# Holding back GpSimd's cast loads in a sparse 3x3 convolution until the weights are on chip

## Chip, cores, metric

One core of one Trainium2 chip. The metric is the device time of one execution in microseconds (us). A profile gives a span, from the first to the last instruction, that is 1.7 to 1.8 us shorter than the time of the same execution.

## The reference

```python
x:      (16, 64, 64, 64)  float32
weight: (128, 64, 3, 3)   float32, about 90% of it zero
x_pad = np.pad(x, ((0, 0), (0, 0), (1, 1), (1, 1)))
output[b, co] = sum over ci, kh, kw of weight[co, ci, kh, kw] * x_pad[b, ci, kh:kh+64, kw:kw+64]
# output: (16, 128, 64, 64) float32
```

The kernel takes no advantage of the zeros and computes a dense convolution in bf16. It reads 17 MB and writes 33.5 MB.

## The kernel before

Images go in eight pairs, 64 channels of each on 128 partitions. Three kinds of loads stand at the start. The SP queue brings the weights and the first 36 rows of pair 0 in fp32 (`x_head`, in two pieces of 9 and 27 rows), which VectorE and ScalarE cast to bf16. GpSimd brings everything else with loads that cast on the way.

```python
nc.sync.dma_start(out=w_sb, in_=weight...)
x_head = const_pool.tile([128, HEAD, W], FP32, name="x_head")          # HEAD = 36
for a, b in ((0, 9), (9, HEAD)):
    nc.sync.dma_start(out=x_head[:, a:b, :], in_=pair(0)[:, a:b, :])
nc.gpsimd.dma_start(out=xs[0][:, HEAD:H, :], in_=pair(0)[:, HEAD:H, :])  # tail of pair 0
...
for p in range(1, NP):
    nc.gpsimd.dma_start(out=xs[p], in_=pair(p))                          # seven more pairs
... # 27 matmuls of zeros, casts and transposes of the weights
cast_x(nc.vector.tensor_copy, 0, 9)      # x_head, first piece
cast_x(nc.scalar.copy, 9, 18)            # x_head, second piece
cast_x(nc.vector.tensor_copy, 18, HEAD)
```

The first 16 rows are two "direct" blocks of 18 matmuls. All other blocks take two output rows at once: GpSimd adds neighbouring rows into `s`, TensorE makes products, and VectorE adds two of them into `o`. When both `o` tiles of a pair are complete, SP stores them (2.1 MB each; the last pair goes in four stores of 1 MB).

## Time and profile before

| | before |
|---|---|
| median of the first three runs | 132.42 us (132.15 to 132.76) |
| span of the trace | 130.3 us |
| second piece of x_head on chip | 13.96 us |
| TensorE without a gap | 14.71 to 117.10 us |
| last addition into o ends | 119.64 us |

The record calls the profiled run (132.03 us) slow. There is only one core, so no second die to hold it against, and the runs beside it took as long. A second trace of the same kernel stands among the experiments (b_again).

These are three rows of the page's table of 40 equal slices, each of 3.26 us here: the clock granted to TensorE in tenths of full speed, the busy share of the 16 DMA engines in tenths, and the GB/s that they wrote.

```profile
PEclk9985559999999999999999999999999999999655
DMA  4999999999999999999999999999599929999990
GB/s 136 217 297 228 216 209 226 209 216 216 302 325 307 327 322 314 362 428 438 423 425 428 433 423 433 428 428 443 244 408 403 403 86 402 458 385 415 415 410 18
```

Two things are to be seen. TensorE has half its clock from the fourth slice to the sixth, around its wait for x_head. The DMA engines are full from the second slice on except in two places late in the kernel, a 5 and a 2, with 244 and 86 GB/s. Such a place, where the engines have too little to do, is called a hole below; its size is the length of the stage times what the share lacks of 1.

### The profile page before, as it was taken

The page shows a single profiled execution, that of the slowest core. Times are in us where ns is not written, and L with a number is a line of the kernel's source. Part 1 is how long each engine was busy: PE and PEld are TensorE (multiplying, and loading weights), DVE is VectorE, ACT ScalarE, POOL GpSimd, SP SyncE. Part 2 cuts the span into 40 slices and gives each one's busy share as a digit, 9 for nine tenths or more (in the row PEclk, how much of TensorE's full clock was granted, in tenths as well). Part 3 has the DMA queues.
Part 4 walks back from the last instruction along what each step waited for, and adds up shares of the span by engine and source line. Part 5 has one row for each costly group of instructions (what it writes and reads, how often), then busy time and mean ns, then how long its engine had stood idle before and what let it go on. Part 6 is the DMA issues. An engine that isn't in the chain of part 4 may idle for free.

```text
span 130.3 us, 2488 instructions
## 1 busy us (share of the span) xinstructions
PE 110.6 (85%) x1002; PEld 56.0 (43%) x1002; DVE 83.0 (64%) x136; ACT 38.0 (29%) x70; POOL 40.7 (31%) x45
## 2 busy tenths in 40 slices
PE   6662499999999999999999999999999999993000
PEld 6430144445444544454445445544544454440000
DVE  0350425778777868787777777777777777777000
ACT  3500313333333333333243333333333333330000
POOL 6900463333333333333333333324333330000000
PEclk9985559999999999999999999999999999999655
DMA  4999999999999999999999999999599929999990
GB/s 136 217 297 228 216 209 226 209 216 216 302 325 307 327 322 314 362 428 438 423 425 428 433 423 433 428 428 443 244 408 403 403 86 402 458 385 415 415 410 18
DMA packets 4188, 42.99 MB, mean 330 GB/s; under 512 B 464, under 2 KB 464, under 8 KB 976
## 3 DMA queue, kind: packets, MB, share of 16 engines
q1 hardware_dynamic: 3024, 35.03, 64.6%
q0 software_dynamic: 1152, 7.80, 29.1%
q8 instruction: 8, 0.13, 0.4%
q14 instruction: 4, 0.03, 0.1%
HBM read 17.07 MB, written 33.55 MB: 389 GB/s over the span
## 4 chain that ended last, share of the span: by engine, by line
PE 79%; DMA 9%; DVE 1%; issue 1%; SPq 1%; ACT 1%; DVEq 0%
PE ps L136 79%; DMA x_head<-in_x_dram 9%; DVE o L169 1%; ACT x L88 1%; DVEq L215 0%; SPq L63 0%; SPq L60 0%; DVEq L169 0%
## 5 line engine op out<-in xcount | busy, mean ns | idle before, releaser
L136 PE MATMUL ps<-x,wT 64*128 64x504 bf16 (+3 forms) x780 | 91.4, 381 | 6.7 <-ACT x L88 4.2
L169 DVE TENSOR_TENSOR o<-ps,pc 128x512 f32<-128x512 f32 x124 | 77.8, 686 | 22.4 <-PE ps L136 20.1
L136 PEld LDWEIGHTS <-wT 64*128 64x128 bf16 x966 | 52.4, 96 | 60.4 <-issue 10.4
L155 POOL TENSOR_TENSOR s<-x 128x512 bf16<-128x512 bf16 x31 | 35.6, 1152 | 65.6 <-PE ps L136 43.4
L162 ACT COPY pc<-ps 128x512 f32<-128x512 f32 x62 | 33.3, 589 | 64.3 <-issue 61.8
L136 PE MATMUL ps<-s,wT 64*128 64x512 bf16 (+1 forms) x186 | 25.8, 380 | 0.0
L88 DVE CAST x<-x_head 128x576 bf16<-128x576 f32 (+1 forms) x2 | 1.2, 611 | 7.5 <-DMA x_head<-in_x_dram 7.5
L75 PE MATMUL ps<-idle_rhs 128*128 128x128 bf16 x27 | 3.1, 313 | 1.0 <-DVE idle_rhs L72 1.0
L68 POOL DMA_DIRECT2D x<-in_x_dram x7 | 3.7, 551 | 0.0
L150 DVE COPY o<-ps 128x512 f32<-128x512 f32 x2 | 1.4, 688 | 3.4 <-PE ps L136 3.4
L75 PEld LDWEIGHTS <-idle_rhs 128*128 128x128 bf16 x27 | 2.8, 149 | 1.0 <-DVE idle_rhs L72 1.0
L88 ACT CAST x<-x_head 128x576 bf16<-128x576 f32 x1 | 0.7, 672 | 8.2 <-DMA x_head<-in_x_dram 8.2
L92 DVE CAST w_bf<-w_sb 128x192 bf16<-128x192 f32 (+1 forms) x4 | 1.2, 360 | 2.5 <-DMA w_sb<-in_weight_dram 2.5
L149 ACT COPY o<-ps 128x512 f32<-128x512 f32 x2 | 1.2, 582 | 3.6 <-PE ps L136 3.6
L92 ACT ACT_TABLE_LOAD x1 | 1.3, 1283 | 0.7 <-PEq L204 0.7
L98 PE MATMUL ps<-ident,w_bf 128*128 128x128 bf16 x9 | 1.2, 308 | 0.0
L92 ACT CAST w_bf<-w_sb 128x64 bf16<-128x64 f32 (+1 forms) x2 | 0.7, 417 | 1.4 <-DMA w_sb<-in_weight_dram 1.4
L102 DVE TENSOR_TENSOR wT<-ps,wT 128x384 bf16<-128x384 f32 x2 | 1.0, 549 | 0.0
L98 PEld LDWEIGHTS <-w_bf 128*128 128x128 bf16 x9 | 0.8, 130 | 0.4 <-DVE w_bf L92 0.4
L64 POOL DMA_DIRECT2D x<-in_x_dram x1 | 0.7, 696 | 0.8 <-POOLq L204 0.8
L72 DVE MEMSET idle_rhs<- 128x64 uint32 x1 | 0.1, 112 | 0.8 <-PEq L204 0.8
L111 ACT CAST wT<-ps 128x384 bf16<-128x384 f32 x1 | 0.5, 478 | 0.4 <-PE ps L98 0.4
(8 smaller groups left out, 1.9 us busy)
## 6 DMA issues: line engine op xcount, KB each, us to landing
out_dram<-o SPq DMA_DIRECT2D x14, 2048.0 KB, 14.4
x<-in_x_dram POOLq DMA_DIRECT2D x7, 1024.0 KB, 26.1
out_dram<-o SPq DMA_DIRECT2D x4, 1024.0 KB, 9.4
x_head<-in_x_dram SPq DMA_DIRECT2D x1, 864.0 KB, 12.3
x<-in_x_dram POOLq DMA_DIRECT2D x1, 448.0 KB, 8.8
w_sb<-in_weight_dram SPq DMA_DIRECT2D x1, 288.0 KB, 2.7
x_head<-in_x_dram SPq DMA_DIRECT2D x1, 288.0 KB, 6.0
```

The lines of the kernel that those rows point to most:

```text
L68: nc.gpsimd.dma_start(out=xs[p], in_=pair(p))
L75: nc.tensor.matmul(idle_ps, idle_rhs, idle_rhs, start=True, stop=True)
L88: copy(out=xs[0][:, a:b, :], in_=x_head[:, a:b, :])
L92: copy(out=w_bf4[:, g, a:b, :], in_=w_v[:, k : k + b - a, :])
L98: nc.tensor.matmul(wps[:, j, :], src, ident, start=True, stop=True)
L102: nc.vector.tensor_tensor(out=wT[:, g], in0=wps, in1=wT[:, G1], op=SUB)
L136: nc.tensor.matmul(ps[n][:, lo:hi, c_lo:c_hi], tap(g, kw, n), src[q, a:b:step, c_lo + kw - 1 : c_hi + kw - 1], start=(i == 0), stop=(i == ...
L149: nc.scalar.copy(out=o[0][:, r0 : r0 + rows, :], in_=ps[0])
L150: nc.vector.tensor_copy(out=o[1][:, r0 : r0 + rows, :], in_=ps[1])
L155: nc.gpsimd.tensor_tensor(out=s, in0=xs[p][:, r0 : r0 + 16 : 2, :], in1=xs[p][:, r0 + 1 : r0 + 16 : 2, :], op=ADD)
L162: nc.scalar.copy(out=c, in_=shared[n])
L169: nc.vector.tensor_tensor(out=o[n][:, first : r0 + 16 : 2, :], in0=ps[n], in1=pc[n], op=ADD)
```

## The change

Its intent: GpSimd issues its cast loads only when the weights are there, so that the weights and x_head have the DMA engines to themselves. To make GpSimd wait for the weights, it takes over one of the small casts.

```diff
-    nc.gpsimd.dma_start(out=xs[0][:, HEAD:H, :], in_=pair(0)[:, HEAD:H, :])
     ident = const_pool.tile([128, 128], BF16, name="ident")
     make_identity(nc, ident)
-    for p in range(1, NP):
-        nc.gpsimd.dma_start(out=xs[p], in_=pair(p))
 ...
     cast(G2, nc.scalar.copy, 0, 3)
-    cast(G2, nc.vector.tensor_copy, 3, 4)
+    cast(G2, nc.gpsimd.tensor_copy, 3, 4)
+
+    nc.gpsimd.dma_start(out=xs[0][:, HEAD:H, :], in_=pair(0)[:, HEAD:H, :])
+    for p in range(1, NP):
+        nc.gpsimd.dma_start(out=xs[p], in_=pair(p))
```

## The prediction

> **What bounds the kernel now.** I read the page's slice table first, then the chain that ended last, then the start in the timeline, then the stages with DMA share. The chain of waits names one wait only, at the start:
>
> ```profile
> 1.65 12.31 DMA x_head<-in_x_dram
> 13.96 0.02 issue
> 13.98 0.68 ACT x L88
> 14.66 0.04 issue
> 14.71 102.39 PE ps L136 x936
> ```
>
> The columns are start and length in us. After the second piece of x_head has landed at 13.96, TensorE works without a gap until 117.10. So the start looks like pure loss, and a chain read alone would promise all of it back. Section 6 of the page says why that piece takes so long:
>
> ```profile
> x_head<-in_x_dram SPq DMA_DIRECT2D x1, 864.0 KB, 12.3
> x<-in_x_dram POOLq DMA_DIRECT2D x1, 448.0 KB, 8.8
> w_sb<-in_weight_dram SPq DMA_DIRECT2D x1, 288.0 KB, 2.7
> x_head<-in_x_dram SPq DMA_DIRECT2D x1, 288.0 KB, 6.0
> ```
>
> Read the last column, us from issue to landing. 288 KB of weights take 2.7, the same amount of x_head behind them 6.0: from 3.5 us on GpSimd's cast loads share the engines. The chain stops at compute, so the DMA needs a look of its own. In this answer by stages the last three columns are the granted clock, the DMA engines' busy share and GB/s:
>
> ```profile
> 20.00:33.00 13.00, 13.00 (x126) 6.50 (x123) 9.92 (x16) 4.45 (x10) 4.80 (x5) 1.00 1.04 214
> 33.00:57.00 24.00, 24.00 (x228) 11.98 (x226) 18.42 (x31) 8.10 (x16) 8.82 (x8) 1.00 1.01 333
> 57.00:91.00 34.00, 34.00 (x320) 16.98 (x318) 26.84 (x43) 11.52 (x22) 12.21 (x11) 1.00 1.01 429
> 91.00:95.00 4.00, 4.00 (x42) 2.02 (x38) 2.87 (x5) 1.37 (x3) 1.62 (x2) 1.00 0.66 272
> 95.00:104.00 9.00, 9.00 (x86) 4.49 (x84) 7.17 (x12) 3.12 (x6) 3.17 (x3) 1.00 0.99 415
> 104.00:107.00 3.00, 3.00 (x34) 1.52 (x30) 2.48 (x4) 0.91 (x3) 0.99 (x2) 1.00 0.04 11
> 107.00:127.00 20.00, 11.28 (x106) 5.43 (x102) 10.04 (x16) 3.48 (x7) 0.45 (x1) 0.86 1.00 418
> ```
>
> The DMA engines are full almost throughout. GB/s counts what is written, so a cast load from fp32 to bf16 shows 214 while it reads twice that, 428, the same as the 429 of pure stores: **some 428 GB/s of the wider side is the ceiling here**. The page gives 17.07 MB read and 33.55 MB written, 50.6 MB, or 118 us of a 130 us span. The engines run dry in just two places, because the outputs are not computed yet: 91 to 95 (4 x 0.35 = 1.4 us) and 104 to 107 (2.9 us). So this kernel has two bounds nearly level: late compute, and the bytes.
>
> **What the Trainium skill says.** "DMA: Bandwidth & Descriptors", section "Issuing engines are not separate DMA queues", says that DMAs of all issuers run on the same 16 engines and interleave; its section "Queues, rings and completion order" says that each engine goes round-robin between queues packet by packet. The trace agrees: 6.0 us against 2.7 us for 288 KB. "TensorE: Matmul & The Clock Gate", section "What's actually happening", says that the array's clock halves after an idle window of about 3.4 us and needs as long a busy one to recover. The trace agrees: after the gap from 10.49 to 14.71 the 18 matmuls of the second direct block take 4.02 us, those of the first, partly at full clock, 2.77. "SBUF — State Buffer", section "SBUF: two separate sides", says that some VectorE copies lock GpSimd out of the port that it writes descriptors through. The trace does not show it: GpSimd's seven issues keep to 535 to 563 ns each though VectorE casts from 3.46 to 4.63.
>
> **The change, part by part.**
> Removed from the start: the 448 KB load (issued at 1.23) and seven loads of 1024 KB (2.46 to 6.19). Added to GpSimd: one cast of 128x64 elements, taken from VectorE, where the smallest cast of that group took 0.21 us. GpSimd took 1.15 us for a two-input add of 128x512, so an eighth of the elements should cost 0.2 to 0.4 us (estimate). It also makes GpSimd wait for the weights.
>
> 1. The loads. Weights land at 3.46, the cast ends near 3.8, the first issue starts there. Before, the first cast packet followed its issue by 2.3 us (1.23 to 3.54), so now **first cast packets near 6.1 to 6.5**, 2.5 to 3 us later. Meanwhile the SP queue is alone: 1.475 MB of weights and x_head. In the stage 2 to 4 us it moved 242 GB/s with 2304 B rows; the 864 KB with 6912 B rows should run near 400. I get x_head's first piece landing near 4.5 to 5.5 and the second near 6.5 to 7.5, not 7.2 and 13.96.
>
> 2. Compute. First direct block from about 5.5 (before 7.72), at half or full clock 1.9 to 4.0 us. The casts of the second piece take 0.67 and 0.76 us, so the second direct block starts near 8 and ends at 10 to 11.5. The first product on s started at 18.50 before. GpSimd's eight issues (0.70 + 3.73 = 4.4 us) run until about 8.3, then 1.15 us for s: 9.5, ready in time. Gain of the compute side: **7 to 8.5 us**, so the last addition into o ends near 111 to 112.5 and not 119.64.
>
> 3. The tail rows of pair 0 must be there when the third block wants s, near 12. They need 0.92 MB at 428 = 2.1 us after 6.3 and about 1.3 us until the wait is released (estimate): 9.7. Pair 1 follows 4.9 us later, 14.6, wanted near 19. Hidden.
>
> 4. The stores start 7 to 8 us sooner, but the bytes are the same. After 6.5 us about 49.1 MB remain, at 427 GB/s 115 us: data until about 121.5 to 122 even with no idle engine. Pair 6's stores would come near 99, when by bytes (42.2 MB loaded and stored before them) the queue is busy until about 102. So **the holes at 91 and 104 close and nothing more can be won**: at most 1.4 + 2.9 = 4.3 us, plus 0.3 at the start, less what the later start of the cast loads costs. Of the 7 to 8 us of compute, 3 to 4 go into a queue.
>
> 5. The hole from 91 to 95 is not a common pause. Narrow stages there:
>
> ```profile
> 91.00:92.00 1.00, 1.00 (x14) 0.50 (x10) 0.46 (x1) 0.29 (x1) 0.47 (x1) 1.00 0.90 369
> 92.00:93.00 1.00, 1.00 (x14) 0.53 (x12) 1.00 (x3) 0.00 (x0) 0.00 (x0) 1.00 0.57 229
> 93.00:94.00 1.00, 1.00 (x14) 0.48 (x12) 1.00 (x2) 0.62 (x2) 0.52 (x1) 1.00 0.12 49
> 94.00:95.00 1.00, 1.00 (x12) 0.51 (x10) 0.42 (x2) 0.46 (x1) 0.64 (x1) 1.00 1.05 442
> ```
>
> The share sinks over three microseconds: some of the 16 engines finish near 91.5, the slowest near 94.4, when the next stores begin. A store is done when its slowest engine is done. That engine loses nothing here; only the hole from about 104.8 to 107.1, 2.3 us, is dead time for it too. If the spread among the engines stays, the saving is nearer to 2.4 than to 4.3. I choose **3.6 us** between: 132.42 - 3.6 = 128.8.
>
> **The rivals.**
> - Compute was the whole bound: the end moves by 7 to 8 us, 124.5 to 125.5. For it: the chain. Against it: the DMA share of 1.0 and 50.6 MB at 428. I give it one in twenty.
> - The slow engines decide: 2 us or less, 130.2. For it: the narrow stages and the last bytes, which trickle from 127 to 128.8 at a share of 0.10 and less. Against it: two engines only trail at the very end, and need not be the ones that were slow before. One in five.
> - GpSimd becomes the wait: it now has weights, cast, eight issues and s in one line, and s may come a microsecond late for the first block of the two-row kind. That costs compute 1 us of 7 to 8, of which 3 are spare against the DMA queue: nothing at the end.
> - The output buffers push back: seven o tiles, each waiting for its earlier store. Before, pair 2's first store landed at 70.0; pair 5 reuses its buffer and now wants it near 75. By bytes it lands near 69 to 70. Nothing, unless stores slip by 5 us.
> - The loads were hidden anyway and only start later: then the DMA engines have a hole near 6 us of up to 0.5 us, counted above.
>
> **Range and chances.** 2.1 us saved (slow engines and a hole at the start) gives 130.3; 5.2 us (all holes, a better start, no trailing engines) gives 127.2. The line of 2% lies at 129.8, that is 2.6 us saved, one below my choice and with the slow-engine case beyond it: 0.78 faster, 0.20 same, 0.02 slower.
>
> **What would show it right or wrong.** Right: x_head's second piece lands before 8; no gap over 3 us in TensorE after 6; the last addition into o ends near 112; the DMA share stays at 1.0 from about 10 to 122 with no hole at 91 or 104; the time from the last addition to the end grows from 10.6 to some 14 us. Wrong: holes that stay (compute did not move, or s waits for GpSimd), a stage with less than 420 GB/s of wider-side traffic (then mixing loads and stores costs bandwidth that I don't count), or a long tail at a DMA share below 0.2 (then the slowest engine took the gain).

## The result

| | before | after |
|---|---|---|
| median | 132.28 us (131.89 to 132.76, 4 runs) | 128.53 us (127.89 to 129.06, 4 runs) |
| span of the trace | 130.3 us | 127.1 us |
| second piece of x_head on chip | 13.96 us | 8.76 us |
| first product on s | 18.50 us | 11.45 us |
| last addition into o ends | 119.64 us | 112.27 us |
| from there to the end of the span | 10.7 us | 14.8 us |

The ratio is 0.9713, with a 95% interval from 0.9652 to 0.9773. A ratio is the mean time of one kernel's fast runs over that of the other's fast runs of the same rounds, so it is not quite the ratio of the medians. The output is correct.

The chain of waits of the changed kernel, start and length in us:

```profile
1.65 7.11 DMA x_head<-in_x_dram
...
9.51 100.22 PE ps L137 x936
```

TensorE's gapless stretch begins 5.2 us sooner. It is also 2.2 us shorter (100.22, before 102.39), because the clock does not fall any more. The issues of the start, with KB and us from issue to landing in the last columns:

```profile
x_head<-in_x_dram SPq DMA_DIRECT2D x1, 864.0 KB, 7.1
x<-in_x_dram POOLq DMA_DIRECT2D x1, 448.0 KB, 7.1
w_sb<-in_weight_dram SPq DMA_DIRECT2D x1, 288.0 KB, 2.9
x_head<-in_x_dram SPq DMA_DIRECT2D x1, 288.0 KB, 3.6
```

x_head's second piece takes 7.1 us and not 12.3, its first piece 3.6 and not 6.0. The clock, DMA share and GB/s of the changed kernel, in slices of 3.18 us:

```profile
PEclk9999999999999999999999999999999999997555
DMA  4799999999999999999999999999999999999980
GB/s 131 214 227 220 217 211 217 217 317 299 333 315 322 340 294 320 340 312 315 333 407 438 423 433 428 420 438 423 438 418 433 418 444 423 415 418 420 433 348 21
```

The stretch at half clock is gone, and so are the two late holes. A third hole, a 7, has come in at the start. The last stages, where the final three columns are clock, DMA share and GB/s:

```profile
91.00:95.00 4.00, 4.00 (x41) 2.07 (x37) 3.27 (x7) 1.07 (x2) 1.15 (x1) 1.00 1.00 426
95.00:104.00 9.00, 9.00 (x88) 4.89 (x86) 6.96 (x13) 3.22 (x6) 2.31 (x2) 1.00 1.02 431
104.00:107.00 3.00, 3.00 (x32) 1.57 (x29) 2.27 (x4) 1.07 (x2) 0.00 (x0) 1.00 1.00 426
107.00:122.00 15.00, 3.92 (x38) 1.87 (x34) 4.55 (x8) 1.07 (x2) 0.00 (x0) 0.79 1.00 423
122.00:124.00 2.00, 0.00 (x0) 0.00 (x0) 0.00 (x0) 0.00 (x0) 0.00 (x0) 0.50 0.65 274
124.00:128.00 4.00, 0.00 (x0) 0.00 (x0) 0.00 (x0) 0.00 (x0) 0.00 (x0) 0.50 0.03 14
```

Where the kernel before had shares of 0.66 and 0.04, this one has 1.00. All arithmetic ends at 112.27, and the engines then work off stores for ten more microseconds. Of 7.4 us that compute gained, 3.2 arrive at the end of the span. (The trace of the kernel before is slow. Against b_again compute gained 5.9 us and the span 1.7.)

### The profile page after: what moved, and what is told of

Its sections match the earlier page's. It is cut to its first block, busy times and chain, and to the rows that moved or that the text cites.

```text
span 127.1 us, 2488 instructions
## 1 busy us (share of the span) xinstructions
PE 108.2 (85%) x1002; PEld 58.6 (46%) x1002; DVE 82.8 (65%) x135; ACT 38.0 (30%) x70; POOL 41.2 (32%) x46
## 4 chain that ended last, share of the span: by engine, by line
PE 79%; DMA 6%; DVE 1%; issue 1%; SPq 1%; ACT 1%; DVEq 0%
PE ps L137 79%; DMA x_head<-in_x_dram 6%; DVE o L170 1%; ACT x L85 1%; DVEq L216 0%; SPq L63 0%; SPq L60 0%; DVEq L170 0%
## 5 line engine op out<-in xcount | busy, mean ns | idle before, releaser
L137 PE MATMUL ps<-x,wT 64*128 64x504 bf16 (+3 forms) x780 | 89.5, 375 | 1.6 <-ACT x L85 1.6
L137 PEld LDWEIGHTS <-wT 64*128 64x128 bf16 x966 | 55.1, 95 | 50.3 <-issue 2.7
```

The lines of the kernel that those rows point to most:

```text
L137: nc.tensor.matmul(ps[n][:, lo:hi, c_lo:c_hi], tap(g, kw, n), src[q, a:b:step, c_lo + kw - 1 : c_hi + kw - 1], start=(i == 0), stop=(i == ...
```

## The experiments

**Theory 1**: the kernel before is set by late compute, the changed one by the bytes through the DMA engines. **Theory 2**: compute sets both, and the rest of its gain is lost in some other way. **Theory 3**: bytes bound both. Twelve kernels ran.

A word on the times. On some chips the kernel before scatters more than in the four runs of the first measurement: 127.39 to 132.72 us in 29 runs on one, 131.11 to 133.11 in 20 on another. Runs over 1.5% above a kernel's fastest are called slow, and of such a spread that rule keeps the low end only. Below I give the medians and ranges of all runs, and the ratio of fast runs where there is one.

### A store less, in both kernels: a_skip and b_skip

```diff
-            for n in range(2):
+            for n in range(1 if p == 3 else 2):
                 nc.sync.dma_start(out=out[2 * p + n], in_=o[n])
```

One image of pair 3 is not written, so the output is wrong.

> The changed kernel without the store of one image of pair 3 (2.1 MB fewer; that image is wrong on purpose). Theory 1, the bytes set the end of the changed kernel: 2.1 MB at 428 GB/s are 4.9 us, of which compute gives way to about 4 (the last addition into o at 112.3, and pair 6's stores at 99 plus the 24 us that the kernel before took from there): 124.0 to 125.2 us. Theory 2, compute still sets the end: no more than 0.5 us below the changed kernel, 128.0 to 128.5.

> The same store left out of the kernel before. Theory 1 says that late compute sets its last stage (pair 6's stores at 106.3 find an empty queue): the holes grow, the end stays, 131.9 to 132.4. Theory 2, that bytes bound both kernels: 4 to 5 us less, about 127.6 to 128.4.

Measured in the same rounds on one chip: a_skip 124.39 us (123.18 to 125.02, 6 runs); b_skip 131.37 (130.98 to 132.35, 6 runs); the kernel before 131.15 (29 runs). The recorded ratios to before, 0.9696 and 1.0268, are both called unclear. a_skip lies in its range of theory 1. b_skip lies half a microsecond below its range, but level with the kernel before beside it; its ratio holds it against the eight runs of that kernel at 127.4 to 128.8, where none of its own six fell. So 2.1 MB less are worth nothing to the usual run of the kernel before, and about 4 us to the changed one (128.53 in the first measurement; it did not run on this chip). The stage where the missing store shows, first in b_skip, then in a_skip:

```profile
91.00:95.00 4.00, 4.00 (x42) 2.18 (x40) 3.42 (x6) 1.07 (x2) 1.16 (x1) 1.00 0.49 201
```

```profile
95.00:104.00 9.00, 9.00 (x88) 4.89 (x86) 6.96 (x12) 3.23 (x6) 2.30 (x2) 1.00 0.83 350
```

In b_skip the old hole has only grown, from a share of 0.66 to 0.49. In a_skip a hole has opened where the changed kernel has 1.02: with fewer bytes its compute is late again, and the end comes 10.6 us after the last addition, as in the kernel before.

### Two microseconds more on TensorE, in both kernels: a_pe and b_pe

```diff
         last = p == NP - 1
+        if p == 4:
+            extra = psum_pool.tile([128, 8, W], FP32, name="ps")
+            for _ in range(10):
+                nc.tensor.matmul(extra, idle_rhs, xs[p][:, 0:8, :], start=True, stop=True)
```

> The changed kernel with ten matmuls of 128x512 more on TensorE ahead of pair 4, about 2.15 us that nobody reads. Theory 1 (bytes): compute has 3 to 4 us to spare, so 0 to 0.4 us more, 128.4 to 129.0. Theory 2 (compute): 2.1 us more, 130.6.

> The same ten matmuls in the kernel before. Theory 1 says that compute sets the start of its last 24 us: 2.0 to 2.2 us more, 134.4. Theory 2, bytes bound both: 0 to 0.5 us more.

Measured in the same rounds as the stores: a_pe 128.00 us (127.66 to 129.76, 22 runs), with a recorded ratio of 1.0015 to the fast runs of before, which on this chip lie at 127.4 to 129; b_pe 132.99 (130.12 to 134.69, 6 runs), 1.8 above the median of before, ratio 1.0191, unclear (its profiled run is called slow). So by its median the kernel before pays for most of the extra work, though six runs that spread over 4.6 us are weak evidence. Its trace fits: the last addition ends 2.7 us later than in the first trace of the kernel before (also slow), of which 0.6 is a later landing of x_head (14.53, not 13.96), and the span is 2.6 longer. The changed kernel pays nothing that can be seen: 128.0 is below the 128.53 of the first measurement. (The unaltered changed kernel did not run on this chip. Its x_head happened to land at 7.20 in this trace, which gave 1.6 us of the 2.15 back to compute.) The stronger evidence is in its trace: the last addition ends at 113.09, later than the 112.27 of the changed kernel, and the span is 126.1, not more than its 127.1.

### The cast alone, the wait alone: b_cast and a_wait

```diff
 b_cast, from the kernel before:
-    cast(G2, nc.vector.tensor_copy, 3, 4)
+    cast(G2, nc.gpsimd.tensor_copy, 3, 4)
 a_wait, from the changed kernel:
-    cast(G2, nc.gpsimd.tensor_copy, 3, 4)
+    cast(G2, nc.vector.tensor_copy, 3, 4)
+    gate = const_pool.tile([128, 1], FP32, name="gate")
+    nc.gpsimd.tensor_copy(out=gate, in_=w_sb[:, 0:1])
```

> The kernel before with only the engine of the one cast changed; GpSimd still issues all loads at the start and casts after them, near 6.2 us. If the order of the loads does it all: as before, within 0.5 us (131.8 to 132.8). If the freed VectorE time matters: 0.2 us and more less.

> The changed kernel with that cast back on VectorE and a one-column copy of the weights on GpSimd, only as a wait ahead of the loads. If the order of the loads does it all: as the changed kernel within 0.5 us (128.0 to 129.0). If the cast on GpSimd matters: 129.5 or more.

Measured on one chip, with the kernel before at 130.82 (127.79 to 132.51, 7 runs): b_cast 131.57 (131.07 to 131.70, 4 runs), a_wait 127.72 (127.62 to 129.51, 4 runs). Both medians lie 0.2 to 0.3 us below the ranges expected, on a chip where the kernel before is 1.5 us faster too. The moved cast wins nothing by itself, and the wait without the cast brings a gain of the size of the whole change (3.1 us in the medians). The order of the loads is the change; the cast is only its lock.

### How long to hold back, and what: a_tail and a_late

```diff
 a_tail, from the changed kernel: the tail load is issued at the start again
+    nc.gpsimd.dma_start(out=xs[0][:, HEAD:H, :], in_=pair(0)[:, HEAD:H, :])
     ident = const_pool.tile([128, 128], BF16, name="ident")
 ...
-    nc.gpsimd.dma_start(out=xs[0][:, HEAD:H, :], in_=pair(0)[:, HEAD:H, :])
 a_late, from the changed kernel: all loads wait for x_head as well
+    gate = const_pool.tile([128, 1], FP32, name="gate")
+    nc.gpsimd.tensor_copy(out=gate, in_=x_head[:, HEAD - 1, 0:1])
     nc.gpsimd.dma_start(out=xs[0][:, HEAD:H, :], in_=pair(0)[:, HEAD:H, :])
```

> The changed kernel with the 448 KB tail load of pair 0 at the start again and only the seven pair loads behind the weights. If bytes set the end, filling the DMA engines between 3 and 8 us gains about 1 us although x_head lands about 1 us later: 127.3 to 128.0. If compute sets it: 129.3 to 129.8, slower by the later x_head.

> The changed kernel with all GpSimd loads held back until x_head's second piece is on chip (issue near 8.8 instead of 3.9). If bytes set the end, the engines stand empty some 3 us longer and the time grows by as much: 131 to 132. If the time is compute's and the order at the start only: the third block waits 2 to 3 us for the tail rows, and nothing else: similar sum, so here the DMA hole and the wait in the trace must tell which.

Measured in the rounds of b_cast and a_wait: a_tail 129.31 (127.34 to 130.60, 4 runs), a_late 133.25 (133.21 to 133.36, 4 runs).

a_tail met neither forecast cleanly: its median lies in the range for compute setting the end, its fastest run in the range for bytes. That fastest run is the profiled one: there x_head landed at 10.53, all arithmetic ended at 114.05, and the span of 125.6 is the shortest of any kernel that moves all the bytes. The engines are fuller early on, as intended. But compute is then close to being late again. The other three runs took 129.19 to 130.60; that compute was late in them is likely and not shown, as none was traced.

a_late is slower than the kernel before, and 1.2 us above the range that I had given. This is the DMA in two of its stages, then TensorE's wait in its timeline (idle time and its releaser in brackets):

```profile
6.00:8.00 2.00, 1.35 (x14) 0.56 (x11) 0.67 (x2) 0.00 (x0) 0.00 (x0) 1.00 0.33 135
8.00:10.00 2.00, 0.79 (x8) 0.45 (x9) 1.36 (x2) 1.16 (x2) 1.48 (x3) 1.00 0.00 0
```

```profile
14.88 1.07 PE L139 MATMUL ps<-s,wT 64*128 64x512 bf16 x6 [3.55 <-POOL s L158]
```

The engines stand idle for over 3 us, and GpSimd, in order, comes to its first s only after eight issues. Both costs are real, and the next table says which one counts: the last addition ends at 117.39, and if that were what mattered the span would be 128.0. It is 131.5. The hole in the DMA decides: the shares lack 4.4 us of work from 2 to 12 us, those of the changed kernel 1.2. These 3.2 us are most of the 4.4 between the two spans; the rest is not accounted for.

### The clock, or the landing: b_warm and a_tail_warm

```diff
                     direct(p, o, r, rows)
+                    if r == 0:
+                        fill = psum_pool.tile([128, 128], FP32, name="ps")
+                        for _ in range(70):      # 40 in a_tail_warm
+                            nc.tensor.matmul(fill, idle_rhs, idle_rhs, start=True, stop=True)
```

> The kernel before with 70 matmuls of 128x128 after its first direct block, some 4 us that nobody reads, so that TensorE does not sit idle while x_head's second piece comes. If half clock costs the second direct block its 2 us (4.02 against 2.12 in the changed kernel) and compute sets the end of this kernel: 2 us less than the kernel before, about 129 to 130 where that has 131 to 132, and less scatter. If only the landing of x_head matters: as before, 131 to 132.

> The kernel with only the seven pair loads held back (a_tail), with 40 matmuls of 128x128 in the same place. a_tail came out at 127.3 to 130.6. If its scatter is the clock falling to half in the wait for x_head, this one stays near its best: 127.0 to 127.8 in nearly all runs. If it is the landing of x_head itself: scatter as before, to 129.5 and more.

Measured on a third chip, with the kernel before at 131.75 (131.11 to 133.11, 20 runs): b_warm 130.08 (128.73 to 132.02, 6 runs), ratio 0.9778, unclear; a_tail_warm 128.56 (127.74 to 129.61, 6 runs), ratio 0.9773, unclear. The second direct block, first in b_cast, which stands for the kernel before, then in b_warm:

```profile
13.77 4.03 PE L136 MATMUL ps<-x,wT 64*128 64x512 bf16 x18 [5.02 <-ACT x L88]
```

```profile
14.27 2.12 PE L136 MATMUL ps<-x,wT 64*128 64x512 bf16 x18 [2.48 <-ACT x L88]
```

Matmuls of zeros that nobody reads make the block 1.9 us shorter, although x_head lands later in this trace. So some 2 of the 7.4 us that the change gave to compute are the clock, and the rest is the landing (13.96 to 8.76). The scatter did not shrink in b_warm, so the clock is not its only source. a_tail_warm met its better forecast (127.0 to 127.8) in one run of six, its traced one. It spread less than a_tail (1.9 us against 3.3), though in few runs and on another chip, and its median is no better than the changed kernel's. It is my attempt at a version that beats both, and it does not.

### Less of x_head: b_head20

```diff
-    HEAD = 36
+    HEAD = 20
```

> The kernel before, all loads at the start as there, but x_head cut from 36 to 20 rows (second piece 11 rows instead of 27, GpSimd's tail load 44 instead of 28 rows). If what cost the time was the amount of x_head that stands in the shared engines, and the bytes set the rest: x_head's second piece lands near 7.5 to 8.5, the tail near 10, no hole in the DMA between 3 and 8 us, 126.3 to 127.5, faster than the changed kernel by about 1 us. If the loads of GpSimd have to be held back for the first rows to come through: 129 to 132.

Measured in the rounds of b_warm: 130.48 us (129.16 to 131.42, 15 runs), ratio 0.9888. The first forecast is refuted; the second, that GpSimd's loads have to be held back, came true. The two pieces of x_head in its trace:

```profile
x_head<-in_x_dram SPq DMA_DIRECT2D x1, 352.0 KB, 10.7
...
x_head<-in_x_dram SPq DMA_DIRECT2D x1, 288.0 KB, 3.5
```

The second piece has 41% of its former bytes, and still takes 10.7 us where the traces with all 27 rows show 11.4 to 12.9. In the trace's single transfers it is 128 packets, one for each partition, in both kernels: 2816 bytes each here and 6912 there. Their own time is short (medians of 0.125 and 0.275 us), while a cast packet takes 0.44 us in the tail load here and 0.62 us in the pair loads. My reading is that an engine serves cast packets between two of x_head's, so that the piece waits for its number of turns more than for its size. This is not shown: the trace does not name the engine of a transfer, the same edit made the tail load longer (44 rows and not 28), and no run gives x_head fewer packets. What the run shows is that asking for less of x_head does not bring it early, while holding the cast loads back does.

### The kernel before against itself: b_again

No edit.

> The kernel before, unchanged, as a control and for a second trace of it; it has scattered from 127.4 to 132.7 us on some chips. If its time follows from when x_head's second piece lands: the span is that landing plus 116.3 to 117.0 us where TensorE falls to half clock (as in four traces of its kind), or plus 114 where it does not (b_warm), and a run of 127.5 us needs a landing before 12. If the trace has a late landing and a short time, something else makes the scatter.

Measured on the chip of a_skip: 131.18 us (129.61 to 132.47, 22 runs) against 131.34 (127.97 to 132.40, 27 runs) of the same kernel. The means of all runs agree (ratio 0.9998), yet the ratio of fast runs is 1.0161, because one lucky run of 127.97 decides which of the others count as fast. In this trace x_head lands at 13.18, TensorE recovers its clock within the second direct block (3.62 us), and the span is 115.6 us longer than the landing, between the two cases that I had set out. The holes are there. From 91 to 107 us they add up to 2.9 us, where the first trace of this kernel has 4.3; the span is shorter by about as much (1.5).

```profile
100.00:105.00 5.00, 5.00 (x51) 2.60 (x48) 4.27 (x8) 1.33 (x3) 1.31 (x2) 1.00 0.57 236
105.00:108.00 3.00, 3.00 (x32) 1.58 (x30) 2.42 (x5) 0.91 (x3) 1.00 (x1) 1.00 0.83 350
```

### All traces in one table

The end of the last addition into o is its start in the timeline plus its length. The first trace of the kernel before, b_pe and b_head20 are of slow runs, the others of fast ones.

| kernel | last addition ends | span | difference |
|---|---|---|---|
| before | 119.64 | 130.3 | 10.7 |
| b_again | 118.19 | 128.8 | 10.6 |
| b_skip | 118.88 | 129.6 | 10.7 |
| b_pe | 122.34 | 132.9 | 10.6 |
| b_cast | 119.19 | 129.8 | 10.6 |
| b_head20 | 118.70 | 129.4 | 10.7 |
| b_warm | 117.04 | 127.6 | 10.6 |
| a_skip | 112.48 | 123.1 | 10.6 |
| after | 112.27 | 127.1 | 14.8 |
| a_wait | 112.01 | 125.8 | 13.8 |
| a_pe | 113.09 | 126.1 | 13.0 |
| a_tail | 114.05 | 125.6 | 11.6 |
| a_tail_warm | 114.84 | 126.0 | 11.2 |
| a_late | 117.39 | 131.5 | 14.1 |

This settles theory 1. In every kernel that issues its loads at the start, and in a_skip with its missing bytes, the end follows the last addition by 10.6 to 10.7 us: compute sets it, by the moment at which the last stores can be issued. In every kernel that holds loads back and moves all the bytes, the difference is larger, and the surplus is time spent in the store queue. The changed kernel's own surplus is 4.2 us.

## Why the prediction was right

It said 128.8 us, and 128.53 was measured. By its steps:

1. **The loads.** x_head's first piece landed at 4.8, as said; the second at 8.76, 1.3 us after the range of 6.5 to 7.5, and past the 8 that I had named as a sign of being right. In the single transfers, nine packets of the piece took 0.9 to 1.7 us instead of 0.26, and while seven of the 16 packets in flight at once had run out by 6.8, the others went on to between 7.7 and 8.5. The landing goes with such slow packets: a_pe has none and landed at 7.20, within my range; a_late (8.46), a_wait (8.49) and a_skip (8.96) have two to four of 0.9 to 2.2 us each. What makes them slow is open. It is not the cast loads beside them: in a_late none ran yet. The first cast packet came at 6.79, not at 6.1 to 6.5: 2.9 us after its issue, where the kernel before had 2.3. One reading of mine was too strong: I took 6.0 against 2.7 us for 288 KB as the effect of sharing. In the changed kernel the same piece takes 3.6 before any cast packet moves, so 0.9 of these 3.3 us is its place behind the weights (whose own load took 2.7 and 2.9).
2. **Compute.** Right. The first product on s came 7.05 us sooner and the last addition 7.4, within 7 to 8.5, and b_warm shows how much of it is the clock. (Against b_again the last addition came 5.9 sooner.)
3. **The tail rows.** They landed at 11.0, not 9.7, and pair 1 near 17.2, not 14.6; why the two were 6.1 us apart and not 4.9 is open. GpSimd's timeline in the changed kernel has both waits:

```profile
9.70 1.15 POOL L156 TENSOR_TENSOR s<-x 128x512 bf16<-128x512 bf16 x1 [1.15 <-DVE x L85]
11.05 2.26 POOL L156 TENSOR_TENSOR s<-x 128x512 bf16<-128x512 bf16 x2 [0.20 <-DMA x<-in_x_dram]
17.19 3.38 POOL L156 TENSOR_TENSOR s<-x 128x512 bf16<-128x512 bf16 x3 [3.88 <-DMA x<-in_x_dram]
```

TensorE shows no gap after 9.51, so both stayed hidden. Pair 1 had less to spare than I had thought: its first s was ready near 18.3, and TensorE took it at 21.09.
4. **The stores.** Right, and the heart of it. The holes closed, compute's surplus went into the queue, and a_skip and a_pe against b_skip and b_pe show it. The term that I took too small is the hole at the start. First the kernel before, then the changed one:

```profile
4.00:6.00 2.00, 1.24 (x10) 0.90 (x10) 0.63 (x3) 1.15 (x3) 2.00 (x5) 1.00 0.86 218
6.00:10.00 4.00, 2.28 (x18) 1.17 (x18) 1.86 (x4) 0.00 (x0) 0.20 (x1) 0.86 1.10 301
```

```profile
4.00:6.00 2.00, 1.87 (x14) 1.07 (x15) 1.85 (x6) 1.32 (x3) 2.00 (x4) 1.00 0.76 206
6.00:10.00 4.00, 2.42 (x22) 0.99 (x20) 1.87 (x4) 1.16 (x2) 2.85 (x6) 1.00 0.91 232
```

With 0.82 from 2 to 4 us as well, the changed kernel loses 0.36 + 0.48 + 0.36 = 1.2 us there; the one before loses 0.3 (0.14 of 2 us). So 4.3 us of closed holes, less 0.9, are 3.4; the spans differ by 3.2. The hole of 1.2 us belongs to this trace and not to the change: counted in the same way, a_wait, a_skip and a_pe, which hold the loads back as well, lose 0.3, 0.3 and 0.1 us, within the 0.5 that I had allowed, and the spans of a_wait and a_pe, which move all the bytes, are 1.3 and 1.0 us shorter. That fits the slow packets of step 1: the traced run had nine, the other three two at most.
5. **The slow engines.** They left their mark, though not as the cause of the missing part: the last bytes of the changed kernel ebb from 122 to 125.5, a share of 0.65 and then 0.03. I took 0.7 us off the 4.3 for this spread, and the hole at the start took 0.9 off. That the sum fits so well is in part luck. How much the spread costs by itself no run separates. As an estimate from the shares, the end of the changed kernel from 122 us on lacks 3.7 us of work, that of the kernel before from 126 on 3.3.

Of the rivals, "compute was the whole bound" is refuted by a_pe and a_skip. "GpSimd becomes the wait" did not come true here (s was ready at 10.85, TensorE took it at 11.45), but does in a_late. The output buffers never pushed back: TensorE has no gap.

**What stays open.** On some chips the kernel before has a few runs at 127.4 to 128.8 us (8 of 29 in one set, 1 of 27, 1 of 7 and 0 of 20 in others), as short as the changed kernel's. By the rule of the table such a run needs its last addition to end near 115 to 116.5 (the time less 1.75 and 10.6), so an early landing of x_head, full clock, or both. No trace of such a run was caught, so this is inferred and not shown. One number points to the clock: the mean granted clock of these ten runs is 0.949 to 0.962, that of every run of this kernel over 130.7 us in the same sets 0.926 to 0.944. That fits less time at half clock; when x_head landed in these runs the record does not say. The gain of 3.75 us in the medians is thus the gain over the usual run; against the luckiest runs of before there is none.

## What to carry to other kernels

When a chain of waits shows only compute, look at the share of the DMA engines in stages, and count holes: here closing holes was all that faster compute could win while the bytes stayed the same. The time from the last arithmetic to the end tells which side sets the end, if one kernel is known where it is compute. A small transfer that is wanted at once should not stand beside big ones on the same engines, and making it smaller may not help: 41% of the bytes landed only 0.7 to 2.2 us sooner. But where the bytes set the end, time in which the DMA engines stand idle while the others are held back is paid at the end (a_late).

## What the Trainium skill lacked or had wrong

- "DMA: Bandwidth & Descriptors", Specifications: it has about 1 us for the first byte of a DMA issued from GpSimd, and does not say what other transfers do to it. From the start of GpSimd's first issue to the first cast packet the traces show 1.4 us where the engines were idle (a_late; 0.7 from the end of the issue), which agrees, but 2.3 (before) and 2.9 (after) beside loads of the SP queue.
- The same page, "Where 436 GB/s comes from": for transfers between HBM and SBUF it has the HBM side bind at about 358 GB/s. Here, in a program on one core, pure stores ran at 429 GB/s for 34 us, and cast loads, counted by what they read, at 428. Its section "Measured" has this right: 425 for one core, about 358 for each with both cores of a pair at work.
- The same page, "Queues, rings and completion order", has the round-robin by packets, but no figure for a small load beside cast loads: 41% of the bytes, as many packets in the trace (one for each partition, while the page's packet is typically 9 to 17 descriptors), 10.7 us instead of 11.4 to 12.9.
- The same page, "Latency and other measured facts", says that two of the 16 DMA engines (7 and 15) are usually slower, without a figure for what that costs at the end of a long stream. In the kernel before the packets in flight fell from 16 to one over some 3 us, from 91.5 to 94.4, and at the end of the changed kernel from 122 to 125.5; both are pure stores. The trace does not name the engines.
